# One more pair of merge-gate columns in the front, and no merge columns beside heads 5 and 6 of the delta rule

## The chip, the cores and the metric

The kernel runs on one core of a Trainium2 chip. The metric is the device time of one execution in microseconds (us); lower is better. Engines are named as in the profile: PE is TensorE (PEld its loads of weights), DVE is VectorE, ACT is ScalarE, POOL is GpSimd, SP is SyncE, which here issues all transfers.

## What is computed

One layer of a hybrid encoder, in float32, over 640 rows: a prompt of 512 tokens and 8 sequences of 16 new tokens.

```python
z = x @ w_in        # q, k, v, f, gate of attention; q|k|v, a, beta, gate of the delta rule; m_a, m_b
y_a = (attention(q_a, k_a, v_a, logf) * silu(gate_a)) @ w_out_fox
q_b, k_b, v_b = split(silu(causal_conv4(qkv_b)))
o_b, s_new = gated_delta_chunked(l2norm(q_b), l2norm(k_b), v_b, g, beta, s0)
y_b = (rms_norm(o_b) * silu(gate_b)) @ w_out_gdn
h = (sigmoid(m_a) * y_a + sigmoid(m_b) * y_b) @ w_out
x1 = layer_norm(alpha * x + h)
x_out = x1 + sigmoid(x1 @ w_pl_gate) * rms_norm(p @ w_pl_proj)
```

The change concerns the product that gives `m_a` and `m_b`, the merge gates: 2 x 2048 columns of `w_in`, in 32 blocks of 128 columns (merge columns below). Each is tanh'd, stored to memory as `md`, and read back in the last part of the kernel.

## The kernel before

All products with large weights are made in split float32: a weight block is loaded as two halves (`wr`, 512 KB each), cut into pieces of 128x512 by `w_piece` (L299) into a rounded `wh` (ACT, L307) and the rest `wl` (DVE, L308), and multiplied as wh.xh + wh.xl + wl.xh. A block of 128 output columns over all 2048 inputs and 640 rows comes in one of two forms:

- a **plain column** (`column`, L364): 16 steps of 6 matmuls of 128x320 (L361 and L362), 96 matmuls;
- a **pair** (`pair`, L414): two blocks at once in seven products of half size, the way of Strassen's scheme, 7 x 8 x 3 = 168 matmuls (L435). It needs 14 pieces instead of 8, sums of weights on DVE (L297) and additions of results.

Pairs need sums of the inputs, which are there in the front alone, so the front works in pairs: 4 pairs of attention gates, 2 of values, FRONT/2 = 10 of merge columns, 2 of attention heads. Then come the attention (`phase_fox`), the delta rule (`phase_gdn`, L1499), and the tail. The 12 merge columns that are not in the front are plain ones and stand beside other work: three in the attention, one behind the four columns (q, v, k, gate) of each of heads 0 to 6 of the delta rule (`FILL`, L1542), and two behind head 7 (tag "cth"), which are followed by the eight columns of the attention's output product.

The order of work is fixed when the program is recorded. Every step of a column ends in a `tick` (L123), in which lanes of generators may record some steps of the attention or the delta rule; a generator says after each step for how many ticks it waits. On the chip, each engine then runs its own instructions in the recorded order and waits by semaphores. Where the recorder needs that a lane has come to some point, it calls `until` (L141), which ticks, without columns in between, until that is so:

```python
def until(self, cond):
    while not cond():
        self.clock += 0.88
        self.tick()
```

The delta rule of a head goes through these steps, head by head, in several lanes at once:

- `conv_silu` (L815): convolution and SiLU on each of q, v and k. Before it writes its result (L836, L841), it waits in the recorder for the buffer: `while self.done[c] < h - 2 + c % 2` (L834); for k (c = 2) of head h that is the mark `done[2]` of head h - 2.
- `gdn` (L846): transposes (L858, L871), decay, the two triangular matrices (L917 to L924), which are stored (`ld`, L936).
- `gdn_blocks` (L931): `lanes` are loaded from `ld` (L939), then 31 sub-steps of forward substitution on DVE (L947 and L949 each, plus one L951 in the first), two to a recorded step.
- `gdn_chunks`, with `gdn_pro` (L1066) for the prompt: four chunks t = 0 to 3 in a chain: the state S is read by L1120 on PE, DVE makes `rp` (L1124), L1128 on PE, ACT makes `vn` (L1130), L1133 on PE, DVE makes the new S (L1138); L1142 and L1143 on PE give the chunk's output. At t = 3, L1120 is what sets the mark `done[2]` (L1122).
- `gdn_out` (L982).

Head 7's gate is evacuated by `silu_evac` (L776 on ACT, L777 and L778 on DVE) and stored (L1531). In the first of the two columns behind head 7, before step 8, `each1` (L1555) calls `until(lambda: not conv["gens"])` (L1557), so that all convolutions are recorded before their last rows are stored (L1558). Independently, POOL makes sums of weights for the tail in batches of four (`weight_sums`, L259: loads L270, sums L274, stores L279).

Of the kernel before, what the change touches and what calls it, by code (L numbers as in the profile page):

```python
# [52 lines left out]
class Kernel:  # L53
# [5 lines left out]


    PIECES = 5
    FRONT = 32 - 5 - 7
    PAIR0, PAIRS = 6, 6 + FRONT // 2 + 2
    BETWEEN = 6,
    APART = 3, 6
    FILL = 1
    GATES = 6
    FREE = 0.5
    LATE = 3
# [1143 lines left out]
    def front(self, work):  # L1213
# [70 lines left out]
        def parts(src, hi, lo):  # L1284
            nc.scalar.copy(out=hi, in_=src)
            nc.vector.tensor_tensor(out=lo, in0=src, in1=hi.bitcast(F32), op=ALU.subtract)
# [86 lines left out]
        def heads(x, hf, z, u=None):  # L1373
# [8 lines left out]

            def close(h=self.APART[n - 6 - self.FRONT // 2]):
                if x == 0:
                    nc.scalar.mul(o, o, FOX_SCALE)
                nc.sync.dma_start(out=self.qkd[h, x], in_=m[x])
                if x:
                    nc.sync.dma_start(out=self.o["fk"][h], in_=m[x])
# [10 lines left out]
        for n in range(self.PAIRS):  # L1399
# [3 lines left out]
            def back(i, k):  # L1403
# [14 lines left out]
                if i == 6:  # L1418
                    hi, lo = self.op[2 * k]
                    parts(tiles[k // 3][:, (k % 3) * HALF:(k % 3 + 1) * HALF], hi[:, xb], lo[:, xb])  # L1420
            self.pair(xf, gates if n < 4 else vals if n < 6 else merges if n < 6 + self.FRONT // 2 else heads, back)
            if n < 4:
                self.ng += 2
            elif 6 <= n < 6 + self.FRONT // 2:
                self.nm += 2
# [73 lines left out]
    def phase_gdn(self, conv, work):  # L1499
        nc = self.nc  # L1500
        re = self.zt([P, T], "dt", 1, "re")
        nc.sync.dma_start(out=re, in_=self.sqd)
        self.eye = self.zt([80, 8, 32], "eye")
        nc.sync.dma_start(out=self.eye.rearrange("p c i -> p (c i)"), in_=self.i["eye"])
        ws = self.zt([P, 684], "ws")
        self.sums["gens"].append(self.weight_sums([ws[:, x:x + 171] for x in range(0, 684, 171)], slice(8, None),
                                                  (10, 8, 5)))
        self.uu = self.zt([P, 5, P], "uu")
        self.t1 = self.zt([64, 4, 64], "t1")
        self.kpad = self.zt([P, 8, 32], "kpad")  # L1510
        self.gpad = self.zt([P, 8, 32], "gpad")
        for x in (self.uu, self.t1, self.kpad, self.gpad):
            nc.gpsimd.memset(x, 0.0)

        self.kqs = [self.zt([P, 2, T], f"kq{i}") for i in range(2)]

        self.ready, self.done = [-1] * 3, [-1] * 3
        self.gdone = -1
        self.scaled, self.chdone = False, -1
        self.ends["gens"].append(self.scale_e(re))  # L1520
        self.untapped = 0
        for h in range(H):
            for c in range(4):
                acc = self.column()[0]
                kq = self.kqs[h % 2]
                if c == 1:
                    v = self.zt([P, T], "v")
                if c == 3:
                    sg = self.zt([P, T], "sg")
                    self.silu_evac(acc, sg, "gth")  # L1530
                    nc.sync.dma_start(out=self.sgd[h], in_=sg)  # L1531
                else:
                    self.until(lambda: self.untapped == 0)
                    ct = 8 * (0, 2, 1)[c] + h
                    self.untapped += 1
                    stp = self.strip_evac(acc, ct)
                    conv["gens"].append(self.conv_silu(stp, ct, h, c,
                                                       v if c == 1 else kq[:, 1 - c // 2, :]))
            if h == 7:
                self.every = 1  # L1540
            work["gens"].append(self.gdn(h, kq, v))
            for _ in range(self.FILL if h < 7 else 0):  # L1542
                self.mcol("sg")


        raw, nop = {}, [None] * KT
        due = deque()

        def load(k, tag):
            raw[k] = self.zt([P, T], tag, 1, "ogr")  # L1550
            nc.sync.dma_start(out=raw[k], in_=self.ogd[k])
            if k < 8:
                due.append((self.now + 8, k))

        def each1(s):  # L1555
            if s == 8:
                self.until(lambda: not conv["gens"])  # L1557
                nc.sync.dma_start(out=self.o["conv"], in_=self.tails)  # L1558
            if s in (8, 10, 12):
                load((s - 8) // 2, tags[(s - 8) // 2])  # L1560
        tags = "strip", "cy", "sg"

        def take():
            k = due.popleft()[1]
            nop[k] = self.split(raw[k])
            if k + 3 < 8:
                load(k + 3, tags[k % 3])

        def after(s):
            if due and due[0][0] <= self.now and due[0][1] <= s:  # L1570
                take()
        self.mcol("cth", each=each1)
        self.mcol("cth", after=after)
        self.op = nop
        self.fd = [self.tc.dram_tile([P, T], F32, name=f"fd{i}") for i in range(16)]
        self.nf = 0

        def kept(ps):
            t = self.zt([P, T], ("strip", "cy")[self.nf % 2], 1, "fx")
            for hf in range(2):  # L1580
                nc.scalar.copy(out=t[:, hf * HALF:(hf + 1) * HALF], in_=ps[hf])
            nc.sync.dma_start(out=self.fd[self.nf], in_=t)
            self.nf += 1
        for n in range(8):
            def each(s):
                while n == 0 and due and (due[0][0] <= self.now or due[0][1] <= s):
                    take()
                k = 8 + n
                if s == 1 and n < 7:
                    self.until(lambda: self.gdone >= n)  # L1590
                    load(k, ("sg", "cth")[n % 2])
                if s == 13 and n < 7:
                    nop[k] = self.split(raw[k])
            self.column(groups=((0, 8), (8, 16)), base=0, each=each, done=kept)
        self.until(lambda: self.gdone == 7 and not self.sums["gens"])
        self.paced = False
# [598 lines left out]
def _layout(a):  # L2195
# [9 lines left out]
    bl = []  # L2205
    m = [x for j in range(16) for x in (ma[j], mb[j])]

    bv = [seg["v"][:, g * 512:(g + 1) * 512].reshape(4, 4, P, 512).transpose(0, 2, 1, 3).reshape(4, P, DM)
          for g in range(1)]
    nf, r = Kernel.FRONT, Kernel.FILL  # L2210
    bl += [bq[0], bk[0], *bv[0]]

    for b in [*bg, *_wblock(seg["v"])[4:], *m[:nf], *[x[h] for h in Kernel.APART for x in (bq, bk)]]:
# [9 lines left out]
    bl += [pj[0], pj[1]]  # L2223
    for h in range(H):
        bl += [gq[h], gv[h], gk[h], gg[h]]
        if h < 7:
            bl += m[nf + 3 + r * h:nf + 3 + r * (h + 1)]
    bl += m[nf + 3 + 7 * r:]
    for n in ("w_out_fox", "w_out_gdn"):
        wo = _wblock(a[n][0])  # L2230
        bl += [np.concatenate([wo[2 * i], wo[2 * i + 1]], 1) for i in range(8)]
# [72 lines left out]
```

## Time and profile before

| | us |
|---|---|
| median of 3 runs | 2193.96 (2193.01 to 2194.24) |
| profiled execution, its own time | 2190.86 |
| its span, first to last instruction | 2188.9 |
| PE busy | 2174.4 |
| DVE busy | 1525.0 |
| ACT busy | 915.7 |
| POOL busy | 295.3 |

The profile is of one execution. A group's line gives its source line, engine and operation, the tiles out<-in, count and duration; in a window's line each engine's busy time is followed by its number of instructions. Matmuls overlap: one of 128x320 is shown with 0.31 us, and the next starts 0.15 us later. A 128x128 product in plain float32 is two matmuls in the trace ("x2").

### The profile page before, as it was taken

To read this page: it belongs to the slowest core of one execution; us is meant where nothing else is said; L and a number is where in the kernel's file an instruction comes from. 1 tells how busy PE (TensorE), PEld (TensorE's weight loads), DVE (VectorE), ACT (ScalarE), POOL (GpSimd) and SP (SyncE) were. 2 spreads that over 40 slices of the span, in tenths; PEclk is the share of its full clock that TensorE was granted. 3 is DMA by queue.
4 is the path that set the end of the run, shared out by engine and by line. 5 is a ranking of instruction groups with operands and counts; after the bars stand their busy time and mean duration, and the time that the engine had idled before them with its cause. 6 is when DMAs were issued, how large, how long until landed. Compare 5 with 4: busy or idle time off the path is not lost.

```text
span 2188.9 us, 41631 instructions
## 1 busy us (share of the span) xinstructions
PE 2174.4 (99%) x15654; PEld 2108.6 (96%) x15654; DVE 1525.0 (70%) x3134; ACT 915.7 (42%) x2042; POOL 295.3 (13%) x510
## 2 busy tenths in 40 slices
PE   9999999999999999999999999999999999999998
PEld 7799999999899999999999999999999999999998
DVE  5877777667445447566776866867635787789987
ACT  4344444444333334334534434435432343354544
POOL 0022333332000000112121211111100000011100
PEclk9999999999999999999999999999999999999999
DMA  6356665666876747734444435446646656674465
GB/s 233 103 185 196 200 190 185 194 206 206 312 249 245 271 158 251 266 107 132 144 118 138 135 97 152 121 118 198 194 157 212 222 161 210 195 269 139 145 232 171
DMA packets 210761, 405.89 MB, mean 185 GB/s; under 512 B 32488, under 2 KB 109368, under 8 KB 210560
## 3 DMA queue, kind: packets, MB, share of 16 engines
q1 hardware_dynamic: 210560, 403.24, 56.9%
q8 instruction: 123, 2.02, 0.4%
q14 instruction: 78, 0.64, 0.1%
HBM read 312.28 MB, written 90.87 MB: 184 GB/s over the span
## 4 chain that ended last, share of the span: by engine, by line
PE 94%; DVE 2%; DMA 2%; ACT 1%; issue 1%; SPq 0%; POOL 0%; ACTq 0%; DVEq 0%; POOLq 0%
PE g L435 32%; PE g L361 25%; PE g L362 25%; PE g L405 2%; PE s L917 1%; PE s L730 1%; PE s L645 1%; PE s L686 1%; PE s L1056 0%; PE s L405 0%; ACT wh L307 0%; PE s L740 0%; DVE wl L308 0%; DMA ws116b<-ws 0%; DMA nb<-rd 0%
## 5 line engine op out<-in xcount | busy, mean ns | idle before, releaser
L308 DVE TENSOR_TENSOR wl<-wr,wh 128x512 fp32r<-128x512 f32 x626 | 435.0, 705 | 307.4 <-ACT wh L307 300.7
L307 ACT CAST wh<-wr 128x512 fp32r<-128x512 f32 x626 | 382.9, 619 | 305.2 <-PE g L362 141.6
L361 PE MATMUL g<-xh,wh 128*128 128x320 f32 (+1 forms) x1248 | 406.3, 326 | 0.4 <-ACT xh L335 0.3
L361 PE MATMUL g<-xl,wh 128*128 128x320 f32 (+1 forms) x1248 | 385.9, 309 | 0.4 <-DVE xl L336 0.3
L362 PE MATMUL g<-xh,wh 128*128 128x320 f32 x1248 | 385.6, 309 | 0.0
L362 PE MATMUL g<-xl,wh 128*128 128x320 f32 x1248 | 385.5, 309 | 0.0
L361 PE MATMUL g<-xh,wl 128*128 128x320 f32 (+1 forms) x1248 | 385.3, 309 | 0.0
L362 PE MATMUL g<-xh,wl 128*128 128x320 f32 x1248 | 385.2, 309 | 0.0
L435 PE MATMUL g<-xh,wh 128*128 128x320 f32 (+1 forms) x992 | 307.6, 310 | 2.0 <-ACT m L1207 1.6
L435 PE MATMUL g<-xl,wh 128*128 128x320 f32 (+1 forms) x992 | 307.3, 310 | 0.6 <-DVE xl L336 0.6
L435 PE MATMUL g<-xh,wl 128*128 128x320 f32 (+1 forms) x992 | 307.2, 310 | 0.0
L361 PEld LDWEIGHTS g<-xh,wh 128*128 128x128 f32 x1248 | 235.0, 188 | 13.5 <-issue 9.3
L362 PEld LDWEIGHTS g<-xh,wh 128*128 128x128 f32 x1248 | 235.1, 188 | 0.9
L361 PEld LDWEIGHTS g<-xl,wh 128*128 128x128 f32 x1248 | 234.8, 188 | 1.0 <-DVE xl L336 1.0
L362 PEld LDWEIGHTS g<-xl,wh 128*128 128x128 f32 x1248 | 234.7, 188 | 0.0
L361 PEld LDWEIGHTS g<-xh,wl 128*128 128x128 f32 x1248 | 234.3, 188 | 0.3 <-DVE wl L308 0.3
L362 PEld LDWEIGHTS g<-xh,wl 128*128 128x128 f32 x1248 | 234.4, 188 | 0.0
L435 PE MATMUL g<-t,wh 128*128 128x320 f32 (+1 forms) x912 | 201.8, 310 | 0.0
L274 POOL TENSOR_TENSOR ws<-ws 128x171 f32<-128x171 f32 (+2 forms) x152 | 117.4, 772 | 603.6 <-DMA ws<-in_w 596.8
L435 PEld LDWEIGHTS g<-xh,wh 128*128 128x128 f32 x992 | 186.7, 188 | 2.8 <-ACT m L1207 2.1
L435 PEld LDWEIGHTS g<-xl,wh 128*128 128x128 f32 x992 | 186.5, 188 | 1.2 <-DVE xl L336 1.1
L435 PEld LDWEIGHTS g<-xh,wl 128*128 128x128 f32 x992 | 186.8, 188 | 0.0
(436 smaller groups left out, 3533.9 us busy)
## 6 DMA issues: line engine op xcount, KB each, us to landing
wr<-in_w SPq DMA_DIRECT2D x259, 512.0 KB
kc<-in_kc SPq DMA_DIRECT2D x32, 512.0 KB
vc<-in_vc SPq DMA_DIRECT2D x32, 512.0 KB
md<-m SPq DMA_DIRECT2D x32, 320.0 KB
t<-md SPq DMA_DIRECT2D x32, 320.0 KB
sr<-in_w SPq DMA_DIRECT2D x18, 512.0 KB
ws<-in_w SPq DMA_DIRECT2D x100, 85.5 KB
ws<-in_w SPq DMA_DIRECT2D x64, 128.0 KB
```

The lines of the kernel that those rows point to most:

```text
L274: nc.gpsimd.tensor_tensor(out=o, in0=x, in1=y, op=op)
L307: nc.scalar.copy(out=hi, in_=src)
L308: nc.vector.tensor_tensor(out=lo, in0=src, in1=hi.bitcast(F32), op=ALU.subtract)
L361: nc.tensor.matmul(ps[0], whl[w], xhl[o][:, a], start=(first and x == 0), stop=(last and x == 2))
L362: nc.tensor.matmul(ps[1], whl[w], xhl[o][:, b], start=(first and x == 0), stop=(last and x == 2))
L405: nc.tensor.matmul(ps, x[:, sl], w, start=(s == 0 and n == 0), stop=(s == 15 and n == 2))
L435: nc.tensor.matmul(ps, a[:, w], b, start=(k == 0 and n == 0 and not more), stop=(k == 7 and n == 2), skip_group_check=True)
L645: nc.tensor.matmul(s1[32 * j:32 * j + 32, :], self.qpad[:, 2 * j + par, :], kc[:, (j % 2) * NPT:(j % 2 + 1) * NPT], start=(par == 0), stop ...
L686: nc.tensor.matmul(od[32 * j:32 * j + 32, 0:P], self.ppad[:, c, 2 * j + par, :], vc[:, o:o + P], start=False, stop=(par == 1 and c == 3), ...
L730: nc.tensor.matmul(ops[:, 0:P], vn[:, kb, :], pT[:, kb * P:(kb + 1) * P], start=(kb == 0), stop=(kb == i))
L917: nc.tensor.matmul(pp[:, o:o + 256].rearrange("p (a b) -> p a b", a=2), kq[:, 0, x], kq[:, :, x], start=True, stop=True)
```

## The change

`FILL` becomes a number for each head: one merge column behind heads 0 to 4, none behind heads 5 and 6, and two behind head 7, which are the two "cth" columns that were there already. The sum of FILL plus the three columns of the attention is what is not in front, so FRONT goes from 20 to 22: an eleventh pair of merge columns. The host's layout of the weights follows.

```diff
-    FRONT = 32 - 5 - 7
+    FILL = 1, 1, 1, 1, 1, 0, 0, 2
+    FRONT = 32 - 3 - sum(FILL)
     PAIR0, PAIRS = 6, 6 + FRONT // 2 + 2
...
-    FILL = 1
...
-            for _ in range(self.FILL if h < 7 else 0):
+            for _ in range(self.FILL[h] if h < 7 else self.FILL[7] - 2):
                 self.mcol("sg")
```

The order moves on each engine from head 5 on. Three places matter. The first is PE at the last chunk (t = 3) of head 5's chain. Before, a state read L1120 stands between matmuls of a column, and the L1128 that follows it comes 24 column matmuls later:

```order
L361 MATMUL g<-xl,wh 128x320
L362 MATMUL g<-xl,wh 128x320
L361 MATMUL g<-xh,wl 128x320
L362 MATMUL g<-xh,wl 128x320
L1120 MATMUL s<-S,kq_9832 128x128
L361 MATMUL g<-xh,wh 128x320
L362 MATMUL g<-xh,wh 128x320
```

Now, in the first column behind head 7, before its step 8:

```order
L361 MATMUL g<-xh,wl 128x320
L362 MATMUL g<-xh,wl 128x320
L1133 MATMUL s<-vn,kt 128x128
L1142 MATMUL s<-S,gr 128x128
L1143 MATMUL s<-vn,qk 128x128
L1120 MATMUL s<-S,kq_10088 128x128
L1128 MATMUL s<-rp,uu 128x128
L361 MATMUL g<-xh,wh 128x320
```

The third chunk's end, L1120 and L1128 of the fourth now stand in a row with no column matmul between them. Between the end of head 7's gate column and this L1133 stand 48 column matmuls and six steps of the same chain.

The second place is DVE around the same chunk (S is its state, rp its result, sx the substitution of head 6). Before:

```order
L947 TENSOR_TENSOR sx_17347<-sx,lanes 80x8x24
L949 TENSOR_TENSOR sx<-sx,sx_17347 80x8x24
L1138 SCALAR_TENSOR_TENSOR S<-S,gl,s 128x128
L826 SCALAR_TENSOR_TENSOR cy<-strip,taps,cy 128x664
L308 TENSOR_TENSOR wl<-wr,wh 128x512
L947 TENSOR_TENSOR sx_17347<-sx,lanes 80x8x23
L949 TENSOR_TENSOR sx<-sx,sx_17347 80x8x23
L947 TENSOR_TENSOR sx_17347<-sx,lanes 80x8x22
L949 TENSOR_TENSOR sx<-sx,sx_17347 80x8x22
L1124 SCALAR_TENSOR_TENSOR rp<-s,negc,vr 128x128
```

Now (ahead of this S stand the nine operations of sub-steps 31 to 28, from the first `sx<-eye,lanes` on):

```order
L1138 SCALAR_TENSOR_TENSOR S<-S,gl,s 128x128
L947 TENSOR_TENSOR sx_17692<-sx,lanes 80x8x27
L949 TENSOR_TENSOR sx<-sx,sx_17692 80x8x27
L947 TENSOR_TENSOR sx_17692<-sx,lanes 80x8x26
L949 TENSOR_TENSOR sx<-sx,sx_17692 80x8x26
L947 TENSOR_TENSOR sx_17692<-sx,lanes 80x8x25
L949 TENSOR_TENSOR sx<-sx,sx_17692 80x8x25
L947 TENSOR_TENSOR sx_17692<-sx,lanes 80x8x24
L949 TENSOR_TENSOR sx<-sx,sx_17692 80x8x24
L1124 SCALAR_TENSOR_TENSOR rp<-s,negc,vr 128x128
L836 SCALAR_TENSOR_TENSOR kq_10088<-cth,cy 128x512
```

Head 6's substitution begins only just before this chunk, eight of its operations stand between S and rp, and the last convolution (L836) follows rp.

The third place is SP, where head 6's lanes are loaded. Before:

```order
L936 DMA ld<-lt 32x5x32 x4
L254 DMA wr<-in_w 128x1024
L939 DMA lanes<-ld 80x1x1024
L1064 DMA out_sts<-st 128x1024
L254 DMA wr<-in_w 128x1024
```

Now:

```order
L254 DMA wr<-in_w 128x1024
L1531 DMA sgd_175<-sg 128x640
L939 DMA lanes<-ld 80x1x1024
L279 DMA ws142S_235<-ws 128x169
L279 DMA ws142b<-ws 128x169
L279 DMA ws142S_236<-ws 128x169
L279 DMA ws142S_238<-ws 128x169
L254 DMA wr<-in_w 128x1024
L270 DMA ws<-in_w 128x171 x4
L1558 DMA out_conv<-tails 128x648
```

The transfer of lanes now stands right behind the store of head 7's gate, and ahead of a batch of weight sums.

More of the change, by code (lines that the diff above doesn't have):

```diff
@@ L2209, in _layout @@
           for g in range(1)]
-    nf, r = Kernel.FRONT, Kernel.FILL
+    nf = Kernel.FRONT
+    m_ = iter(m[nf + 3:])
     bl += [bq[0], bk[0], *bv[0]]
@@ L2225, in _layout @@
         bl += [gq[h], gv[h], gk[h], gg[h]]
-        if h < 7:
-            bl += m[nf + 3 + r * h:nf + 3 + r * (h + 1)]
-    bl += m[nf + 3 + 7 * r:]
+        bl += [next(m_) for _ in range(Kernel.FILL[h])]
     for n in ("w_out_fox", "w_out_gdn"):
```

## Prediction

> **What bounds the kernel now.** I read the page first, then what TensorE (PE) itself waits for, then busy time by stretch. The page's first lines and the chain that ended last:
>
> ```profile
> span 2188.9 us, 41631 instructions
> ...
> PE 2174.4 (99%) x15654; PEld 2108.6 (96%) x15654; DVE 1525.0 (70%) x3134; ACT 915.7 (42%) x2042; POOL 295.3 (13%) x510
> ...
> PE 94%; DVE 2%; DMA 2%; ACT 1%; issue 1%; SPq 0%; POOL 0%; ACTq 0%; DVEq 0%; POOLq 0%
> ```
>
> PE is busy for 99% of the span and carries 94% of the chain. The longest of PE's own waits (total, times, longest):
>
> ```profile
> PE g L435 <- ACT m L1207: 1.6, 1, 1.6
> ```
>
> It lies in the front. Now stretches, with busy time and number of instructions per engine: the delta rule's heads, their end, one plain column of 96 matmuls, one pair of 168 (three matmuls of a neighbour overlap each of the last two):
>
> ```profile
> core 0: us, PE busy (x) PEld busy (x) DVE busy (x) ACT busy (x) POOL busy (x), PEclk, DMA share, GB/s
> 850.00:1500.00 650.00, 650.00 (x4833) 630.94 (x4832) 458.06 (x1230) 269.72 (x758) 108.37 (x262) 1.00 0.47 143
> 1500.00:1640.00 140.00, 140.00 (x1086) 134.46 (x1086) 82.22 (x231) 62.00 (x160) 16.19 (x30) 1.00 0.60 191
> 889.91:904.02 14.11, 14.11 (x99) 14.11 (x98) 10.48 (x14) 4.66 (x9) 3.23 (x6) 1.00 0.99 336
> 255.98:280.65 24.67, 24.67 (x171) 24.67 (x170) 15.95 (x21) 9.78 (x19) 6.28 (x8) 1.00 0.73 235
> ```
>
> In the delta stage PE has no idle time: 790 of 790 us. So a matmul less is time less, and a PE wait that the change makes is time more. A change of 0.2% (4.4 us) is about what a measurement of this kernel can tell from none.
>
> **What is removed and added.** Two columns go: 2 x 14.11 = 28.22 us of PE. One pair comes: 24.67 us. PE saves 3.55 us, 24 matmuls of 0.147. What a pair needs beside PE (14 casts and subtractions of weight pieces where two columns have 8, three weight sums, additions out of PSUM, two stores) is already in the pair's row: DVE 15.95 and ACT 9.78 of 24.67 us, so it stays under PE's 24.67 us, as it does in the ten such pairs that stand in front now. I cost it at nothing; with the cover gone it would be at most the row's 15.95. The loads of the weights (four halves of 512 KB either way) and the two stores of gates move with the columns, from SyncE's (SP's) queue beside the delta rule to the same queue in front, so what stands behind them there gets through sooner.
>
> **What loses its cover.** Heads 5 and 6 have 14.11 us of columns less each, so the delta rule of head 5 is less far when head 7's columns end. The first merge column after them stops at its step 8 (L1557) until the convolutions are all recorded, and head 7's last one waits (L834) for head 5's fourth state read, L1120. Before, that had been recorded by then. After, the missing steps are recorded there with no matmul of a column between them: the order above shows L1133, L1142, L1143, L1120, L1128 in a row, where 24 column matmuls stood between L1120 and L1128 before. PE must there wait out two DVE results, S (for L1120) and rp (for L1128); all later columns are queued behind. And DVE has eight substitution operations (L947/L949) of head 6 ahead of rp, and nine ahead of S, the first of which waits for a transfer.
>
> PE's own steps, of head 4, as the chain has them:
>
> ```profile
> 1370.17 0.22 PE s L1133 x2
> ...
> 1370.62 0.22 PE s L1143 x2
> ...
> 1372.61 0.22 PE s L1120 x2
> ```
>
> DVE's, of the same time (start, duration):
>
> ```profile
> 1370.43 0.35 DVE L1138 SCALAR_TENSOR_TENSOR S<-S,gl,s 128x128 f32<-128x128 f32 x1 [0.38 <-PE s L1133]
> 1370.70 0.40 DVE L947 TENSOR_TENSOR sx<-eye,lanes 80x248 f32<-80x248 f32 x1
> 1371.13 0.41 DVE L949 TENSOR_TENSOR sx<-eye,sx 80x248 f32<-80x248 f32 x1
> 1371.47 0.17 DVE L951 SCALAR_TENSOR_TENSOR sx<-sx,eye 80x8 f32<-80x8 f32 x1
> 1371.67 0.41 DVE L947 TENSOR_TENSOR sx<-sx,lanes 80x240 f32<-80x240 f32 x1
> ...
> 1372.86 0.35 DVE L1124 SCALAR_TENSOR_TENSOR rp<-s,negc,vr 128x128 f32<-128x128 f32 x1 [0.35 <-PE s L1120]
> ...
> 1374.54 0.39 DVE L947 TENSOR_TENSOR sx<-sx,lanes 80x232 f32<-80x232 f32 x1
> 1374.97 0.40 DVE L949 TENSOR_TENSOR sx<-sx,sx 80x232 f32<-80x232 f32 x1
> ...
> 1377.36 0.38 DVE L949 TENSOR_TENSOR sx<-sx,sx 80x216 f32<-80x216 f32 x1
> 1377.77 0.37 DVE L947 TENSOR_TENSOR sx<-sx,lanes 80x208 f32<-80x208 f32 x1
> ...
> 1380.68 0.35 DVE L947 TENSOR_TENSOR sx<-sx,lanes 80x192 f32<-80x192 f32 x1
> 1381.07 0.35 DVE L949 TENSOR_TENSOR sx<-sx,sx 80x192 f32<-80x192 f32 x1
> ```
>
> From start to start: the first pair of sub-steps takes 0.43 + 0.34 + 0.20 + 0.44 + 0.43 = 1.84 us, the second 4 x 0.43 = 1.7, so S starts 3.55 us after the first L947. The next operation starts 0.27 us after S; eight of 0.41 to 0.39 take 3.2; rp takes 0.35. So L1128 can start 0.27 + 3.2 + 0.35 = 3.8 us after S started, 7.4 us after the first L947.
>
> When does that one start? It needs the lanes transfer (L939), which SP issues right behind the store of head 7's gate (L1531); the gate's first activation (L776) stands on ACT behind an L1130. Rows of head 6 (L1128 and its L1130), then the path of head 0's gate, then head 0's lanes:
>
> ```profile
> 1536.49 0.38 PE L1128 MATMUL s<-vr,uu 128*128 128x128 f32 x2
> ```
>
> ```profile
> 1536.91 0.37 ACT L1130 ACTIVATE vn<-s,cs 128x128 f32<-128x128 f32 x1 [3.41 <-PE s L1128]
> ```
>
> ```profile
> 904.04 0.44 ACT L776 ACTIVATE sc<-g 128x320 f32<-128x320 f32 x1 [3.04 <-PE g L361]
> ```
>
> ```profile
> 907.16 0.32 SPq L1531 DMA_DIRECT2D sgd<-sg  x1
> 907.53 0.42 SPq L800 DMA_DIRECT2D es<-es  x1
> ```
>
> ```profile
> 956.89 0.83 SPq L939 DMA_DIRECT2D lanes<-ld  x1
> ```
>
> ```profile
> 962.41 0.41 DVE L947 TENSOR_TENSOR sx<-eye,lanes 80x248 f32<-80x248 f32 x1 [0.56 <-DMA lanes<-ld]
> ```
>
> Head 0's activation starts as its column ends (904.04 against the window's 904.02). In the new order an L1128 follows the column's end and its L1130 comes first on ACT: 0.42 us to its start and 0.37 long, so the activation starts some 0.7 us after the end. The store goes out 3.1 us later, the next transfer on SP at 3.5. From issue to the DVE operation that waited for it: 962.41 - 956.89 = 5.5 us. So lanes are there 0.7 + 3.5 + 5.5 = 9.7 us after the column's end. PE gets there sooner: 48 column matmuls of 0.147 (7.05 us) and six small steps of 0.22 stand before L1133, and L1133 to L1120 are four more: 7.05 + 10 x 0.22 = 9.25 us of work. L1128 can start at 9.7 + 7.4 = 17.1. The wait is 7.85 us.
>
> POOL may lengthen it. Its sums of weights, four at a time, beside the same DVE operations of another head:
>
> ```profile
> 1544.89 2.68 POOL L274 TENSOR_TENSOR ws<-ws 128x171 f32<-128x171 f32 x4 [14.95 <-DMA ws<-in_w]
> ```
>
> ```profile
> 1545.33 0.63 DVE L947 TENSOR_TENSOR sx<-sx,lanes 80x232 f32<-80x232 f32 x1
> 1545.99 0.56 DVE L949 TENSOR_TENSOR sx<-sx,sx 80x232 f32<-80x232 f32 x1
> ```
>
> 0.63 and 0.56 where 0.39 and 0.40 stood, 0.4 us more for two; about four of them run beside one batch, 0.8 us. In the new order the loads that feed such a batch (L270) stand six places behind lanes on SP, so a batch falls into the stretch; I take 0.8, between 0 and 0.8. [...]
>
> So the wait is 7.85 + 0.8 = 8.65 us and the sum -3.55 + 8.65 = +5.1 us. The profiled execution took 2190.86 us (span 2188.9 and 1.96 around it): 2195.96 after. The median of the runs is 3.1 above the profiled one: 2193.96 + 5.1 = 2199.1.
>
> Bounds: if lanes lie ready when PE comes and POOL keeps out, the wait is 6.1 us (second rival). The other way, two more transfers issued ahead of lanes (0.42 us each, the row at 907.53) and one more DVE operation of the 0.63 kind ahead of S make 1.5 us.
>
> **Rivals.** First, PE's clock falls in the wait. The wait is two gaps of about four microseconds with L1120's 0.22 us between. PE never waited over 1.6 us, so only the two ends of the program show it: the last matmul, the clock in the final stretch, the warm-up at the start, and later matmuls as wide as that:
>
> ```profile
> 2181.10 0.30 PE L435 MATMUL g<-xh,wl 128*128 128x320 f32 x1
> ```
>
> ```profile
> 2186.00:2188.90 2.90, 0.00 (x0) 0.00 (x0) 0.00 (x0) 0.00 (x0) 0.00 (x0) 0.59 0.15 57
> ```
>
> ```profile
> 1.17 4.02 PE L1240 MATMUL wu<-z 128*128 128x512 bf16 x9 [1.17 <-DVE z L1237]
> ```
>
> ```profile
> 41.03 2.95 PE g L405 x12
> ```
>
> A granted clock of 0.59 means that it fell in that stretch, 5 us or so after the last matmul; and after idling the first nine took 0.45 us each against 0.25, so half pace lasts about 4 us and costs 2. [...] It gives 2199.1 + 2 = 2201.1.
>
> Second, not slower: the cover holds better than I count. The place is the start of the first L947; how the first one of each head waited for lanes, in the tile's view:
>
> ```profile
> its engine sat idle before it (us, times) until:
>   DMA lanes<-ld: 0.6, 1
> ```
>
> Seven of eight did not wait at all. If lanes lie ready three matmuls before L1133 here too, at 7.05 + 6 x 0.22 - 0.44 = 7.9 us, L1128 can start at 15.3, the wait is 6.1 us and without POOL the sum is +2.5: 2196.5, no measurable change. For it: those seven. Against: here fewer matmuls stand between L939 and the first L947. It decides from a wait under 7.9 us.
>
> Third, nothing waits, since the recorder's estimate of these gaps was right in all the rest (790 of 790 us busy): -3.55, 2190.4. For it: every other step that PE needs was ready. Against: the five steps stand together in PE's own queue, so some wait must be. To be measurably faster it would need a microsecond more from somewhere.
>
> **How the numbers follow.** My case 0.42, of which 0.30 lies above 4.4 us (slower) and 0.12 below (same); the clock's fall 0.30, slower; the smaller wait 0.22, same; no wait 0.06, half same and half faster. So slower 0.60, same 0.37, faster 0.03. The likeliest is 2199.1. The range goes from the smaller wait less 2 us, a part of the way to no wait (2194.5), to the clock's fall with the 1.5 us of the upper bound (2202.6).
>
> **What would show it.** PE's waits in the changed profile should list L1120 waiting for DVE S and L1128 waiting for DVE rp, some 8 to 9 us together, in the first merge column behind head 7, with lanes as what DVE waits for just before; PE should have 24 matmuls fewer and one pair more at 0.147. A granted clock under 1.00 in the 10 us behind would show the first rival. The forecast is wrong if those two waits sum to under 4 us, or if PE waits elsewhere by more than 1 us.

## The result, and the profile after

| | before | after |
|---|---|---|
| median, us | 2193.49 (4 runs, 2190.89 to 2194.24) | 2204.66 (4 runs, 2202.87 to 2205.52) |
| profiled execution, us | 2190.86 | 2204.55 |
| its span, us | 2188.9 | 2202.8 |

The ratio is 1.0051 (95% interval 1.0039 to 1.0063): the change makes the kernel 11 us slower. The forecast, 2199.1 with a range up to 2202.6, had the sign right and less than half of the size.

The page of the changed kernel opens so:

```profile
span 2202.8 us, 41621 instructions
...
PE 2175.3 (99%) x15630; PEld 2107.9 (96%) x15630; DVE 1539.1 (70%) x3149; ACT 920.0 (42%) x2049; POOL 288.2 (13%) x510
```

Span less busy time is PE's idle time: 14.5 us before (2188.9 - 2174.4), 27.5 now. So 13.0 of the 13.9 us by which the span grew are idle time. PE's busy time grew by 0.9, although PE has 24 matmuls (3.5 us) less to do: it must have worked slowly somewhere. PE's longest waits (total, times, longest):

```profile
PE g L361 <- DVE xl L336: 5.1, 4, 4.2
PE s L1128 <- DVE rp L1124: 3.7, 1, 3.7
PE s L1120 <- DVE S L1138: 3.4, 1, 3.4
```

The lower two are the wait that was forecast. The first one is not: its 4.2 us end some 38 us later. The chain of the work that ended last shows the forecast wait row by row (start, duration):

```profile
1485.56 0.32 SPq L1531
1486.06 4.87 DMA lanes<-ld
1490.95 0.42 DVE sx L947
...
1494.47 0.26 DVE S L1138
1494.73 0.60 DVE sx L947
...
1498.69 0.27 DVE rp L1124
1499.01 0.79 PE s L1128 x2
1499.80 0.27 PE g L361
1500.07 0.27 PE g L362
1500.33 0.27 PE g L361
```

The store of head 7's gate, lanes behind it, the nine substitution operations, S, eight more, rp, then PE. The last three rows show something else: column matmuls start 0.27 us apart, where they start 0.147 apart elsewhere. The windows say why (PE's busy time and number of instructions, the granted clock, the DMAs' share and rate):

```profile
core 0: us, PE busy (x), PEclk, DMA share, GB/s
1486.00:1495.50 9.50, 5.74 (x39) 1.00 0.76 233
1495.50:1502.30 6.80, 3.29 (x14) 0.50 0.39 116
...
1536.50:1539.80 3.30, 3.23 (x12) 0.50 0.40 51
```

The clock fell to half twice, once in each wait, and came back after 6.8 and 3.4 us. PE had work for 3.3 us of each stretch (1499.0 to 1502.3, and 1536.57 to 1539.87) and did about half of it: by the halved clock, as an estimate, 1.65 us lost each time, 3.3 together. The rest of the later wait, again from the chain:

```profile
1524.04 5.52 DMA ogr<-ogd
1529.59 0.73 ACT xh L335
...
1532.13 0.38 DVE ss L893
...
1535.20 0.17 DVE cs L898
1535.72 0.81 DVE xl L336
1536.57 0.63 PE g L361
```

The first output column of the attention needs the eight reloaded attention outputs (`ogr`, L1551), each split into xh on ACT (L335) and the rest xl on DVE (L336). The last xl runs at 1535.72, and PE waits for it from 1532.4 to 1536.57. Its input was ready 4 us earlier:

```profile
1530.74 0.72 ACT L335 CAST xh<-ogr 128x640 fp32r<-128x640 f32 x1
```

What stood in front of it on DVE were head 7's seventeen small operations (L893 to L902, with the `rsqrt` of L186 to L192), 1532.06 to 1535.7. In the kernel before they had run ahead of the first of the eight splits:

```profile
1504.63 0.16 DVE L893 TENSOR_SCALAR ss<-ss 128x10 f32<-128x10 f32 x1
1508.18 1.55 DVE L336 TENSOR_TENSOR xl<-ogr,xh 128x640 fp32r<-128x640 f32 x2
```

Why they moved: `gdn` of head 7 waits at its start in the recorder (`while not self.scaled or self.chdone < h - 2 or min(self.ready) < h`, L848). The third condition asks for head 7's convolutions, the second for head 5's chunks, and the chunks are the last to come. Head 5's chunks had lost 28 us of columns, so head 7 was recorded later against the columns, and its small operations slid past seven splits to stand in front of the eighth.

The theory after the result: four things add up, the pair's saving (-3.5), the wait at the stop (7.1), the wait for the last split (4.2), and the clock (3.3). Rivals: the second wait is due to the late load and not to the small operations; the slow clock costs nothing beyond the waits; the heads are simply short of columns, so a wait that is cured comes back elsewhere; DVE has no time for denser heads, whatever the order.

### The profile page after: what moved, and what is told of

Read it like the earlier page. It is cut to its first block, busy times and chain, and to the rows that moved or that the text cites. A ratio compares the mean times of both kernels' runs of the same rounds, so it can differ in the third digit from the quotient of the medians.

```text
span 2202.8 us, 41621 instructions
## 1 busy us (share of the span) xinstructions
PE 2175.3 (99%) x15630; PEld 2107.9 (96%) x15630; DVE 1539.1 (70%) x3149; ACT 920.0 (42%) x2049; POOL 288.2 (13%) x510
## 4 chain that ended last, share of the span: by engine, by line
PE 92%; DVE 3%; DMA 3%; ACT 1%; issue 1%; SPq 0%; POOL 0%; ACTq 0%; DVEq 0%; POOLq 0%
PE g L435 33%; PE g L361 24%; PE g L362 24%; PE g L405 2%; PE s L917 1%; PE s L730 1%; PE s L645 1%; PE s L686 1%; PE s L1056 0%; PE s L405 0%; DVE wl L308 0%; PE s L740 0%; ACT wh L307 0%; DMA ws116b<-ws 0%; PE s L1128 0%
## 5 line engine op out<-in xcount | busy, mean ns | idle before, releaser
L362 PE MATMUL g<-xl,wh 128*128 128x320 f32 x1216 | 376.1, 309 | 0.0
L362 PE MATMUL g<-xh,wh 128*128 128x320 f32 x1216 | 376.1, 309 | 0.0
L362 PE MATMUL g<-xh,wl 128*128 128x320 f32 x1216 | 375.8, 309 | 0.0
L361 PEld LDWEIGHTS g<-xh,wh 128*128 128x128 f32 x1216 | 229.4, 189 | 13.9 <-issue 8.9
L274 POOL TENSOR_TENSOR ws<-ws 128x171 f32<-128x171 f32 (+2 forms) x152 | 108.9, 717 | 597.3 <-DMA ws<-in_w 582.8
```

Of the source, the lines that this page charges most:

```text
L274: nc.gpsimd.tensor_tensor(out=o, in0=x, in1=y, op=op)
L361: nc.tensor.matmul(ps[0], whl[w], xhl[o][:, a], start=(first and x == 0), stop=(last and x == 2))
L362: nc.tensor.matmul(ps[1], whl[w], xhl[o][:, b], start=(first and x == 0), stop=(last and x == 2))
```

## The experiments

Each was timed beside the kernel before, whose median was 2193.14 us in the first four and 2192.66 in the last four, against 2193.49 beside the changed kernel. So differences from the changed kernel are taken from the ratios: a ratio's 0.001 is 2.2 us, and the changed kernel stands at 1.0051. The profile of each is that of one execution.

### The stop moved from step 8 to step 15

```diff
-            if s == 8:
+            if s == 15:
                 self.until(lambda: not conv["gens"])
                 nc.sync.dma_start(out=self.o["conv"], in_=self.tails)
-            if s in (8, 10, 12):
-                load((s - 8) // 2, tags[(s - 8) // 2])
-        tags = "strip", "cy", "sg"
+            if s in (8, 10, 15):
+                load((8, 10, 15).index(s), tags[(8, 10, 15).index(s)])
+        tags = "sg", "strip", "cy"
```

> The changed kernel, but the stop before the convolution rows are stored stands at step 15 instead of step 8 of the first column behind head 7 (the first three reloads go to the buffers in the order sg, strip, cy, the third with the stop). The recorder then makes no tick without a column there; it makes 8 at the very end of the delta rule instead. Theory (the waits stand where they are seen, and each is a local one): the waits for S and rp (3.4 + 3.7 us) and the first fall of the clock (about 1.7) go, and since head 7's small operations (L893 to L902) now stand behind the last split, the second wait (4.2) with its fall (1.7) goes too: 2204.7 - 8.8 - 5.9 = 2190. Rival (the cover is short by a fixed amount and comes back wherever the recorder next runs out of columns): a wait of 5 to 13 us for the last steps of head 7's chain at the end of the delta rule, 2195 to 2203.

2194.43 us, ratio 1.0008 (0.9999 to 1.0017): 9.4 us of the 11 are gone, and no difference from the kernel before can be measured. PE's waits between 1480 and 1700 us:

```profile
PE s L1120 <- DVE S L1138: 1.7, 1, 1.7
PE s L1005 <- ACT ob L1000: 1.1, 1, 1.1
```

Of the waits that the theory would remove, 1.7 us for S stays (lanes come no earlier), and the end of head 7 brings a new one of 1.1 at L1005. In this execution the granted clock stays at 1.00 through the stop:

```profile
1486.00:1495.00 9.00, 7.30 (x52) 1.00 0.82 233
1495.00:1503.00 8.00, 7.81 (x56) 1.00 0.56 181
```

It is the shortest of the eleven. Six of the eleven have a mean granted clock of 0.998 and take 2195.4 us on average; the five with 0.999, this one among them, take 2193.8. The 1.6 us between are about the price of one fall. That is a hint and no more: the mean also holds the stretch behind the last matmul (a granted clock of 0.59 over the last 2.9 us of the kernel before), and no trace of the six is kept.

The result lies between the theory (2190) and the rival, and by size nearer to the rival's lower end (2195). The rival's mechanism, a wait of 5 to 13 us at the end of the delta rule, did not come: the larger part of the loss was local, and 1.1 us of missing cover come back there.

### Head 7's small operations behind the last split

```diff
         nc.scalar.activation(gr, gr, AF.Exp)
-        yield
+        yield 6 if h == 7 else 1
```

> The changed kernel, but head 7's seventeen small DVE operations (L893 to L902) are recorded five ticks later, behind the last split of the attention outputs instead of in front of it. Theory: the first wait (7.1 us and the clock's fall) stays; of the second wait (4.2 us, for xl of the last split) the 3.6 us of those operations go and with it the clock's second fall (1.7): 2204.7 - 5.3 = 2199.4. Rival: the second wait is due to the late load of the attention outputs (5.5 us from issue), then xl is waited for as before, 2204 to 2205. Second rival: head 7 is late by the five ticks and the time comes back at the end of the delta rule, 2203 to 2205, with a wait there.

2198.7 us, ratio 1.0027 (1.0016 to 1.0038), 5.3 us less than the changed kernel, as the theory had it. The first wait is as it was; of the second this is left between 1500 and 1700 us:

```profile
PE g L361 <- DVE xl L336: 0.8, 2, 0.5
```

On DVE the last split now stands first, behind the same late load (in the changed kernel the seventh split, the first row here, starts at 1530.35):

```profile
1530.41 0.82 DVE L336 TENSOR_TENSOR xl<-ogr,xh 128x640 fp32r<-128x640 f32 x1 [3.12 <-ACT xh L335]
...
1531.97 1.07 DVE L336 TENSOR_TENSOR xl<-ogr,xh 128x640 fp32r<-128x640 f32 x1
...
1535.09 0.20 DVE L893 TENSOR_SCALAR ss<-ss 128x10 f32<-128x10 f32 x1
```

So nearly all of the second wait came from what stood in front of the split, not from the load. Nor did the time come back at the end of the delta rule, though the recorder makes three ticks without a column there.

### No substitution recorded at the stop

```diff
-    def tick(self):
+    def tick(self, skip=None):
...
-            if q["gens"] and q["wake"] <= self.now and q["t"] <= self.clock and (
+            if q is not skip and q["gens"] and q["wake"] <= self.now and q["t"] <= self.clock and (
...
-    def until(self, cond):
+    def until(self, cond, skip=None):
...
-            self.tick()
+            self.tick(skip)
...
-                self.until(lambda: not conv["gens"])
+                self.until(lambda: not conv["gens"], self.blocks)
```

> The changed kernel, but in the ticks without a column at the stop before the convolution rows are stored the substitution of head 6 is not recorded: behind S stands rp at once on DVE, where eight substitution operations stood; seven of them (and with them the wait for lanes) still stand in front of S. Theory: the wait for S stays at 3 to 3.5 us, the one for rp falls from 3.7 to about 0.8; the gap is then too short for the clock to fall: -2.9 - 1.7 = 2200.0, if the second wait stays (head 7's small operations stand in front of the last split here too). Rival (the wait is PE's own chain, not what stands in front on DVE): rp is waited for 3 us or more, 2203 to 2205. The substitution is recorded up to seven ticks later, and the recorder makes six ticks without a column at the end of the delta rule: if that comes back there, 2 to 5 us more.

2202.87 us, ratio 1.0043 (1.003 to 1.0055). PE's waits between 1480 and 1600 us:

```profile
PE g L361 <- DVE xl L336: 4.5, 1, 4.5
PE s L1120 <- DVE S L1138: 3.5, 1, 3.5
PE s L1128 <- DVE rp L1124: 0.4, 1, 0.4
```

The wait for rp falls from 3.7 to 0.4: it was the eight substitution operations in front of rp, as forecast, and not PE's own chain. The wait for S stays, since lanes and the first operations stand in front of it. The time fell by less than that, some 2 us, for three reasons: the expectation that the clock would hold was wrong, for one gap of 3.5 us was enough (0.50 from 1495.3 on, in the window below); 1.0 us came back at L1005 at the end of head 7; and the wait for the last split is 0.3 us longer.

```profile
1495.30:1498.60 3.30, 2.85 (x12) 0.50 0.53 155
```

### The two columns taken from heads 1 and 2

```diff
-    FILL = 1, 1, 1, 1, 1, 0, 0, 2
+    FILL = 1, 0, 0, 1, 1, 1, 1, 2
```

> The changed kernel with the two missing columns taken from behind heads 1 and 2 instead of 5 and 6 (FILL = 1, 0, 0, 1, 1, 1, 1, 2). The recorder makes five ticks without a column at the stop instead of seven. S has been made before the L1120 in that row, with nothing but column matmuls of several steps between, and four substitution operations stand in front of rp. Theory (the wait is what DVE has in front of S and rp): no wait for S, one of about 2 us for rp, no fall of the clock in it; the second wait stays, since head 7's small operations stand in front of the last split: 2204.7 - 5 - 1.7 = 2198. Rival (the missing columns cost the same wherever they are taken): 2203 to 2206. Second rival: heads 1 and 2 wait for their own cover, which shows as waits of PE between 950 and 1150 us.

2195.53 us, ratio 1.0011 (1.0002 to 1.0019), 8.8 us less than the changed kernel. The waits, from 1100 to 1200 us and then from 1480 to 1600 us, are

```profile
PE s L1120 <- DVE S L1138: 3.5, 1, 3.5
```

```profile
PE g L361 <- DVE xl L336: 2.6, 1, 2.6
PE s L1128 <- DVE rp L1124: 1.3, 1, 1.3
```

The second rival is right in part: at 1152 us a wait of 3.5 us for S opens, where there was none. The stop costs 1.3 instead of 7.1, and the second wait 2.6 instead of 4.2. So the cost does depend on where the columns are taken, and heads 5 and 6 were a bad place: 7.4 us of waits here against 11.3 there, and two stretches of half clock of 3.4 us instead of 6.8 and 3.4. The profiled execution is the longest of the eleven (2198.6 us, 3.1 above their median), so its waits may be larger than is usual.

### The waits filled with matmuls that nobody reads

```diff
+    def warm(self, pd, n=16):
+        clock, x = self.clock, self.op[0][0]
+        for _ in range(n):
+            self.nc.tensor.matmul(pd[:, P:P + HALF], x[:, 0:P], x[:, 0:HALF], start=True, stop=True)
+        self.clock = clock
...
                 pd = self.sps()
+                if h == 5 and t == 3:
+                    self.warm(pd)
                 nc.tensor.matmul(pd[:, 0:P], kq[:, 0, tl], s, start=True, stop=True)
...
             pd = self.sps()
+            if h == 5 and t == 3:
+                self.warm(pd)
             nc.tensor.matmul(pd[:, 0:P], uu[:, t, :], rp, start=True, stop=True)
...
+                if n == 0 and s == 7:
+                    self.warm(self.sps(), 20)
+                    self.banks.pop()
```

> The changed kernel with 52 extra matmuls of 128x320 whose results nobody reads: 16 in front of the L1120 and 16 in front of the L1128 at the stop, 20 in front of the matmul that waits for the last split. All other instructions stand as before. They take 2.35, 2.35 and 2.9 us of waits of 3.4, 3.7 and 4.2 us, so the waits end when they did, and no gap is longer than about 1.3 us. Theory (the clock halves in gaps of this length, and the slow stretch after each costs half its 3.3 and 3.4 us): granted clock 1.00 throughout, 2204.7 - 3.4 = 2201.3. Rival (the slow clock costs nothing that the waits don't cover): 2204.7.

2201.0 us, ratio 1.0038 (1.0024 to 1.0051): more matmuls and less time. The two intervals overlap, so the size rests on the trace. Its clock by windows:

```profile
1486.00:1495.00 9.00, 7.76 (x56) 1.00 0.83 237
1495.00:1503.00 8.00, 6.80 (x48) 1.00 0.28 94
...
1532.00:1540.00 8.00, 6.72 (x46) 1.00 0.45 120
```

The clock never falls. By the ratios the time is 2.8 us shorter, where 3.3 were lost to the clock. PE's busy time agrees: it is 4.8 us above the changed kernel's (2180.1 against 2175.3), while 52 matmuls of 0.147 are 7.6, so the rest of PE's work takes 2.8 us less. The slow clock has a price of its own, beside the waits.

### A step in every tick from head 3 on

```diff
-            if h == 7:
+            if h == 3:
                 self.every = 1
```

> The changed kernel, but the lanes may record a step of the delta rule in every tick from head 3 on, instead of in every second one until head 7: the delta rule is then further ahead when the columns run out, and the recorder makes no tick without a column, neither at the stop nor at the end of the delta rule. Theory (the loss is a lag of the recorded order against the columns, not a lack of engine time): both waits go and the pair's saving is left: 2193.3 - 3.5 = 2190. Rival (DVE is too busy beside these heads, whatever the order): waits for DVE in several places between 1150 and 1650 us, 2195 to 2203.

2188.52 us, ratio 0.998 (0.9971 to 0.9988): 4 us faster than the kernel before, with the very columns of the change. Its page:

```profile
span 2187.1 us, 41628 instructions
...
PE 2171.5 (99%) x15630; PEld 2105.1 (96%) x15630; DVE 1532.8 (70%) x3149; ACT 921.4 (42%) x2049; POOL 296.1 (14%) x510
```

PE is idle for 15.6 us, 12 us less than in the changed kernel, and busy 2.9 us less than before, near the pair's 3.5. No wait of PE shows between 1400 and 1700 us. So DVE, at 70% either way, has time enough for the denser heads; it was the lag of the recorded order that cost.

### The same pace in the kernel before

> The kernel before with the same pace (a step in every tick from head 3 on): it had no tick without a column and no wait, so by the theory there is nothing to gain: 2193, within 2 us. Rival (the pace itself is worth something or costs something, whatever the columns): 2190 or below, or 2196 or above; then the run of the changed kernel with this pace is to be set against this one.

2194.29 us, ratio 1.0007 (0.9998 to 1.0016): nothing to gain without the change, as the theory had it. With this pace in both, the pair and the two columns fewer are worth 5.8 us by the medians (2194.29 - 2188.52) and 4.5 in the profiled executions' spans (2191.6 - 2187.1), 3.2 of it PE's busy time (2174.7 against 2171.5). What goes beyond the pair's 3.5 was not traced.

### Heads 1 and 3 without columns, at that pace

```diff
-    FILL = 1, 1, 1, 1, 1, 0, 0, 2
+    FILL = 1, 0, 1, 0, 1, 1, 1, 2
...
-            if h == 7:
+            if h == 3:
                 self.every = 1
```

> The changed kernel with the two missing columns taken from heads 1 and 3 (FILL = 1, 0, 1, 0, 1, 1, 1, 2) and a step in every tick from head 3 on. The recorder makes no tick at the stop and one at the end of the delta rule. Theory (lag only): 2193.3 - 3.5 + 0.9 = 2190.7. Rival (the wait for S moves to where the cover is now missing, as with heads 1 and 2, where 3.5 us came at 1152 us): a wait of 3 us or more in the head after 3 and its clock fall: 2194 to 2196.

2191.84 us, ratio 0.9999 (0.999 to 1.0007). One wait, between 1250 and 1300 us, and the clock around it:

```profile
PE s L1028 <- issue: 2.1, 1, 2.1
```

```profile
1270.00:1275.40 5.40, 3.57 (x59) 1.00 0.32 109
1275.50:1278.80 3.30, 3.11 (x24) 0.50 0.78 252
```

The rival had the kind of loss right (a wait where the cover is missing, with a fall of the clock), with another instruction and a smaller size: 2.1 + 1.6 us, about its distance (3.3 us) to the version with the same pace and the columns of the change. What L1028 waited for the profile does not show.

## Why the prediction was wrong

**The wait at the stop: right.** L1128 was to start 17.1 us after the end of head 7's gate column, 17.9 with the 0.8 taken for POOL. The column's last matmul was followed by the next PE instruction at 1481.78, and L1128 started at 1499.01, 17.2 us on. Within it lanes took 4.9 us to the first L947 instead of 5.5, and S followed that after 3.45 instead of 3.55. One batch of POOL's weight sums ran behind S:

```profile
1494.54 2.35 POOL L274 TENSOR_TENSOR ws<-ws 128x171 f32<-128x171 f32 x4 [27.00 <-DMA ws<-in_w]
```

Beside it four operations of DVE took longer:

```profile
1494.40 0.34 DVE L1138 SCALAR_TENSOR_TENSOR S<-S,gl,s 128x128 f32<-128x128 f32 x1
1494.65 0.67 DVE L947 TENSOR_TENSOR sx<-sx,lanes 80x216 f32<-80x216 f32 x1
1495.35 0.55 DVE L949 TENSOR_TENSOR sx<-sx,sx 80x216 f32<-80x216 f32 x1
1495.94 0.60 DVE L947 TENSOR_TENSOR sx<-sx,lanes 80x208 f32<-80x208 f32 x1
1496.57 0.54 DVE L949 TENSOR_TENSOR sx<-sx,sx 80x208 f32<-80x208 f32 x1
```

They took 2.36 us, where four of 0.39 take 1.56: 0.8 more, the value taken. Counted from start to start, as the sum counts, the stop cost 17.2 - 9.25 = 8.0 us, where the sum had 8.65. The waits of the profile add up to 7.1: they begin where the matmul before them is shown to end (0.39 us for L1143, 0.49 for L1120, where the sum took 0.22), and PE was 0.4 us later at L1133 than the sum had it.

**The step that failed: the sum ended at the stop.** The part "What loses its cover" followed head 5's chain to rp and L1128, and put what stands behind them at nothing, without a reason. It did not ask who waits for head 5's end in the recorder (head 7, by L848) and what head 7's operations would then stand in front of. The text's own condition for being wrong, that PE waits elsewhere by more than 1 us, came true: 4.2 us for the last split, and the fall of the clock behind it, where the sum had nothing. The second experiment shows that the place of these seventeen operations was the cause: with them behind the split, 0.5 us are left of that wait.

**The rival on the clock was true, and twice.** The sum kept the clock at full speed; the rival had 0.30 and 2 us. That in the kernel before the clock fell only some 5 us after the last matmul (1.00 up to 2186.4 us, 0.50 from 2186.6 on) does not speak against it: gaps of 3.5 us and less were enough (below). Nor did L1120 between the two gaps prevent the fall: it was shown to end at 1495.28, and the granted clock is 0.50 from 1495.5 on. The rival's 2 us came from the first nine matmuls of the program, where the granted clock reads 1.00 (1.17 to 5.19 us), so no run shows a fall of that price; here each fall cost some 1.65 us, by the estimate above.

**The pair: right in count, hidden in the sum.** 24 matmuls fewer are in the page. That the saving is real the version with the faster pace shows: with no wait between 1400 and 1700 us, PE is busy 2.9 us less than before.

By size: -3.5 for the pair, 8.0 at the stop, 4.2 at the last split, 3.3 for the clock, together 12.0 us. The medians lie 11.2 apart. The spans of the two profiled executions lie 13.9 apart; three shorter waits for xl (5.1 us in four, above) are 0.9 of that, and as the profiled execution of the kernel before is 2.6 us under the median of its runs, the rest is within what single runs differ by.

**What stays open.** That a cured wait partly comes back at the end of the delta rule is seen in two experiments (1.1 and 1.0 us at L1005), but 5.3 us of what the first experiment was expected to gain did not come, and 2.8 us of it show as waits (1.7 and 1.1). In six of its eleven runs a fall of the clock may be a further part; the rest was not traced.

## What to carry to other kernels

Where work that covers a chain is taken away, follow everything that starts when the chain ends, not only the first wait: an order that is recorded against a clock slides as a whole, and short operations can come to stand in front of something urgent. Price a wait of PE with the half-speed stretch that can follow it (here 3.4 us of half clock and, as estimated, 1.65 us lost, after waits of 2.1 to 4.5 us). And where the engines still have time (DVE at 70%), a lag is cured by letting the order run ahead earlier, here with one number, rather than by giving the cover back; which columns are left out still counts at that pace (3.3 us between the two choices).

## What the hardware showed

Half clock (a granted clock of 0.50) came in stretches of 3.4 us (6.8 where two waits came in a row, in the changed kernel and with head 7's operations behind the split). They began (the seven whose start a window gives) between 0.3 us before and 0.8 us after the end of the wait (of the first wait, where two come in a row). They followed waits of 2.1 us (heads 1 and 3) to 4.5 us (no substitution at the stop); after waits of 1.7 us or less (the profiled run of the stop at step 15, the filled waits, the front's 1.6) the clock stayed at 1.00. What sets the start and the length of a stretch was not shown. For the gap of 2.6 us, in the kernel with heads 1 and 2 without columns:

```profile
1531.70:1535.00 3.30, 3.30 (x14) 0.50 0.78 196
```

PE is busy in the whole of that stretch: the clock fell when the wait was over already, and the time was lost on work alone.
